# Values of four heads at a time: two weight tiles of 512 rows by 512 columns for each group of four

## The chip, the cores and the metric

The kernel runs on one core of a Trainium2 chip. The time is the device time of one execution in microseconds (us), and the number compared is the median of several executions. TensorE (PE) multiplies matrices; VectorE (DVE), ScalarE (ACT) and GpSimd (POOL) do the work on elements; SyncE (SP) issues the DMA transfers between the chip's main memory (DRAM here) and the on-chip memory. Each engine runs its own instructions in a fixed order and waits where a semaphore tells it to. TensorE writes its products to PSUM, which has eight banks of 128 x 512 float32.

## The reference, cut to what matters

512 tokens of 1024 numbers go through two layers (causal attention with forget gates, "fox", then retention), each with twelve heads of 128 and four heads that attend to a memory of 256 rows, and then through a second block: dilated attention in three groups of four heads, a causal convolution of 31 taps, gates, and a feed-forward part. Everything is float32.

```python
q, k, v, f_logit, q_mem, z = split_cols(h @ fox_w_in, [1536, 1536, 1536, 12, 512, 2048])
main = fox_attention(q, k, v, f_logit, fox_b_f)            # 12 heads of 128
...
q, k, v, q_mem, z = split_cols(h @ ret_w_in, [768, 768, 1536, 512, 2048])
main = retention(q, k, v)
...
q, k, v, glu_in, gates = split(h @ w_in, [1536, 3072, 4608, 6656])
for g, (window, dilation) in enumerate(((128, 1), (512, 4), (2048, 16))):
    o[g], m[g], l[g] = dilated_group_attention(q[4g:4g+4], k[4g:4g+4], v[4g:4g+4])
w = l * exp(m - max over groups of m)
a = sum(w * o) / sum(w)
```

The change concerns how the three matrices `v` are computed: 512 x 1024 times 1024 x 1536, once in each of the two layers and once in the second block.

## The kernel before

A float32 operand is held as the sum of two float32r arrays, hi and lo, and a product is three matmuls: hi by hi, hi by lo, lo by hi. Weights arrive in tiles of 1 MB at most. A tile lands in one of two buffers (`ring_w`, loaded from line 314), is split into hi (ACT, line 324) and lo (DVE, line 326) in one of two other buffers (`ring_hl`), and is then used by its "units": pieces of TensorE work of some 5.5 us. All other buffers of 128 x 512 come from two pools, `arena_r` for split and `arena_f` for whole operands. The driver (`run_jobs`) goes through the list of tiles. Before each unit it splits a piece of a coming tile (`cut_ahead`), and after it calls `run_bg`, which emits one step of the waiting background chains (two, if eight or more steps are pending, or if the rate is set to two) and one part of the convolution (up to six taps, line 1418 on DVE). A background chain is, for instance, the attention of one head: scores, exponentials, transposes, products with the values. So what a head's steps hide behind is given by the units that happen to follow. A scheduler may then still move instructions on each engine by its own estimate of times.

Products whose result is wanted with the tokens along the free dimension (queries, keys, gates) hold a 128 x 128 piece of weights and move 512 tokens (`mm3`, lines 213 to 215). Values are wanted the other way round, tokens on partitions. `add_nat` (lines 422 to 424) therefore holds a 128 x 128 piece of x and moves weights: for each tile of 1024 rows by 256 columns, that is two heads, four blocks of 128 tokens by eight row chunks by three, 96 matmuls of 256 columns in two units. The same helper computes the values of the memory heads. Fox calls it through `add_v` once for each of six pairs of heads (in `pair`), retention likewise (in `add_ret`), and the second block through `add_v2` for three groups by two pairs, all three at j = 0 and all three at j = 2 of the loop over the four heads j of a group.

In retention the chain of head h begins with `s1`, four products of the form 128 x 256 to 128 x 512 by two matmuls each (lines 1127 and 1128, the second with 64 rows only), and both heads of a pair are pushed at once.

In the second block head j of the three groups is joined by `push_softmax(j)`. The dilated groups hold the tokens in another order, so the row maxima and sums of all groups go through DRAM (`swap`, lines 1541, 1542, 1547 and 1548: `xn` carries the first group's numbers, `xp` the others'), then the weights of the groups are worked out on DVE (`coef`, lines 1554 to 1563), POOL multiplies the exponentials with them (line 1570), and only then TensorE transposes them (`tr`, line 1585) and multiplies by the values. The last scores before that are those of the first group (`scores_band`), four products by three matmuls on 128 x 256; line 1525 on DVE reads them. The values of the dilated groups go through DRAM too (`vdr`, stored from line 1676, loaded from line 1682).

## Time and profile before

| | before |
|---|---|
| median of 3 runs | 1933.24 us (1933.07 to 1943.24) |
| profiled execution, span | 1935.2 us |
| PE busy | 1880.0 us, 97%, 9759 matmuls |
| DVE busy | 1133.0 us, 59% |
| ACT busy | 826.5 us, 43% |
| POOL busy | 361.5 us, 19% |
| DMA | 194.57 MB, mean 101 GB/s |

The profile is of another execution than the three that were timed; its span, 1935.2 us, is the time that it shows for itself, and no other is given for it. A matmul's busy time is from its start to a modelled end, and neighbours overlap, so the time that a matmul takes is read from the distance between starts. The profile also has the clock that the chip granted to TensorE in each stretch, as a share of its full speed; a share between the two levels (0.50, that is 1.2 GHz, and 1.00, that is 2.4 GHz) is a mean over the stretch.

### The profile page before, as it was taken

The numbers are of one execution on the slowest core, as the hardware profiler recorded it, in microseconds if no ns is written. First come the engines' busy times: TensorE is split into PE (matmuls) and PEld (weight loads), VectorE is DVE, ScalarE is ACT, GpSimd is POOL, SyncE is SP. The second block draws the span as 40 slices with busy tenths as digits, with TensorE's granted clock in tenths as the row PEclk, the third lists the DMA queues.
The fourth block names the chain that finished last, engine by engine and source line by source line (L and its number), as shares of the span: only waits on it lengthen the run. The fifth ranks groups of instructions, "written<-read, shape, count | busy, mean of one in ns | idle before, by whom it ended". The sixth has DMA issues, their size and how long they took to land. (4 is left out here: it accounts for less than half of the span.)

```text
span 1935.2 us, 24633 instructions
## 1 busy us (share of the span) xinstructions
PE 1880.0 (97%) x9759; PEld 1594.7 (82%) x9759; DVE 1133.0 (59%) x1752; ACT 826.5 (43%) x1389; POOL 361.5 (19%) x348
## 2 busy tenths in 40 slices
PE   8999999999999999999999997999899999999998
PEld 7788888888888888888777986988788887888886
DVE  7644443443574564745469796868365387545555
ACT  6544343444445534445244333234353356433342
POOL 1110000111121223223351202020121232100101
PEclk9999999999999999999989998999999999999999
DMA  6341322223242222322223522353453222323221
GB/s 205 120 130 67 98 82 88 92 77 109 87 130 89 77 88 77 94 60 97 66 88 114 166 90 62 80 155 88 136 174 126 98 66 82 116 96 98 98 87 66
DMA packets 200373, 194.57 MB, mean 101 GB/s; under 512 B 22199, under 2 KB 171574, under 8 KB 200258
## 3 DMA queue, kind: packets, MB, share of 16 engines
q1 hardware_dynamic: 200258, 193.00, 32.0%
q8 instruction: 76, 1.25, 0.3%
q14 instruction: 39, 0.32, 0.1%
HBM read 182.40 MB, written 12.94 MB: 101 GB/s over the span
## 5 line engine op out<-in xcount | busy, mean ns | idle before, releaser
L213 PE MATMUL psum<-arena_r,ring_hl 128*128 128x512 f32 (+1 forms) x1936 | 750.1, 388 | 1.8 <-ACT arena_r L1904 1.3
L215 PE MATMUL psum<-arena_r,ring_hl 128*128 128x512 f32 (+1 forms) x1936 | 742.1, 384 | 5.1 <-DVE ring_hl L326 5.1
L214 PE MATMUL psum<-arena_r,ring_hl 128*128 128x512 f32 (+1 forms) x1936 | 742.5, 384 | 3.4 <-DVE arena_r L627 2.6
L326 DVE TENSOR_TENSOR ring_hl<-ring_w,ring_hl 128x1024 fp32r<-128x1024 f32 (+2 forms) x306 | 392.6, 1290 | 314.5 <-ACT ring_hl L324 303.6
L324 ACT CAST ring_hl<-ring_w 128x1024 fp32r<-128x1024 f32 (+2 forms) x307 | 316.1, 1037 | 504.3 <-PE psum L214 335.1
L215 PEld LDWEIGHTS psum<-arena_r,ring_hl 128*128 128x128 f32 x1936 | 367.1, 190 | 77.7 <-DVE ring_hl L326 6.3
L214 PEld LDWEIGHTS psum<-arena_r,ring_hl 128*128 128x128 f32 x1936 | 367.8, 190 | 73.7 <-DVE arena_r L627 3.3
L213 PEld LDWEIGHTS psum<-arena_r,ring_hl 128*128 128x128 f32 x1936 | 367.5, 190 | 73.1 <-issue 2.1
L422 PE MATMUL psum<-ring_hl,arena_r 128*128 128x256 f32 x640 | 183.3, 286 | 2.2 <-ACT ring_hl L324 2.2
L424 PE MATMUL psum<-ring_hl,arena_r 128*128 128x256 f32 x640 | 182.6, 285 | 0.3 <-DVE ring_hl L326 0.3
L423 PE MATMUL psum<-ring_hl,arena_r 128*128 128x256 f32 x640 | 182.5, 285 | 0.0
L1418 DVE SCALAR_TENSOR_TENSOR arena_f<-cpad,vec,arena_f 128x512 f32<-128x512 f32 x240 | 173.3, 751 | 1.7
L422 PEld LDWEIGHTS psum<-ring_hl,arena_r 128*128 128x128 f32 x640 | 124.2, 194 | 3.5 <-ACT ring_hl L324 2.6
L424 PEld LDWEIGHTS psum<-ring_hl,arena_r 128*128 128x128 f32 x640 | 124.1, 194 | 0.6 <-DVE ring_hl L326 0.6
L423 PEld LDWEIGHTS psum<-ring_hl,arena_r 128*128 128x128 f32 x640 | 124.1, 194 | 0.5
L206 DVE TENSOR_TENSOR arena_r<-psum,arena_r 128x512 fp32r<-128x512 f32 (+2 forms) x136 | 79.1, 605 | 71.3 <-ACT arena_r L205 71.1
L205 ACT CAST arena_r<-psum 128x512 fp32r<-128x512 f32 (+2 forms) x136 | 66.9, 526 | 85.0 <-PE psum L215 35.9
L205 ACT CAST arena_r<-arena_f 128x512 fp32r<-128x512 f32 (+1 forms) x78 | 46.2, 598 | 116.8 <-POOL arena_f L1950 67.3
L926 POOL TENSOR_SCALAR arena_f<-arena_f,small 128x512 f32<-128x512 f32 (+3 forms) x48 | 33.9, 726 | 307.9 <-DVE small L924 302.6
L206 DVE TENSOR_TENSOR arena_r<-arena_f,arena_r 128x512 fp32r<-128x512 f32 (+1 forms) x78 | 53.2, 688 | 59.8 <-ACT arena_r L205 59.1
L606 POOL TENSOR_TENSOR arena_f<-arena_f 128x512 f32<-128x512 f32 x40 | 63.6, 1602 | 109.1 <-ACT arena_f L601 106.8
L1950 POOL TENSOR_TENSOR arena_f<-arena_f 128x512 f32<-128x512 f32 x22 | 32.0, 1455 | 262.2 <-DVE arena_f L1926 252.2
(237 smaller groups left out, 2099.3 us busy)
## 6 DMA issues: line engine op xcount, KB each, us to landing
ring_w<-in_fox_w_in SPq DMA_DIRECT2D x28, 1024.0 KB
ring_w<-in_w_in SPq DMA_DIRECT2D x22, 1024.0 KB
ring_w<-in_w_up SPq DMA_DIRECT2D x22, 1024.0 KB
ring_w<-in_w_out SPq DMA_DIRECT2D x20, 1024.0 KB
ring_w<-in_ret_w_in SPq DMA_DIRECT2D x16, 1024.0 KB
ring_w<-in_w_in SPq DMA_DIRECT2D x24, 512.0 KB
ring_w<-in_w_down SPq DMA_DIRECT2D x10, 1024.0 KB
ring_w<-in_w_mem_kv SPq DMA_DIRECT2D x8, 1024.0 KB
```

The costliest lines, as they stand in the source:

```text
L205: nc.scalar.copy(h, src)
L206: nc.vector.tensor_sub(l, src, h.bitcast(F32))
L213: nc.tensor.matmul(ps, wh, xh, start=start and k == 0, stop=False, **o)
L214: nc.tensor.matmul(ps, wh, xl, start=False, stop=False, **o)
L215: nc.tensor.matmul(ps, wl, xh, start=False, stop=stop and k == n - 1, **o)
L324: nc.scalar.copy(j.hv[sl], v[sl])
L326: (nc.gpsimd if j.done in j.spare else nc.vector).tensor_sub(lo, v[sl], j.hv[sl].bitcast(F32))
L422: nc.tensor.matmul(o, c.h[:, sl], h[:, k, :], start=k == 0, stop=False)
L423: nc.tensor.matmul(o, c.l[:, sl], h[:, k, :], start=False, stop=False)
L424: nc.tensor.matmul(o, c.h[:, sl], l[:, k, :], start=False, stop=k == n - 1)
L606: nc.gpsimd.tensor_add(acc, acc, t.ap)
L1418: nc.vector.scalar_tensor_tensor(t, src, wk, t, ALU.mult, ALU.add)
```

## The change

A new helper `add_wide` computes the values of four heads from two tiles of 512 rows by 512 columns (1 MB each, as before). A matmul holds the same 128 x 128 piece of x and moves 512 columns of weights. The products of the four token blocks, 128 x 512 each, stay in four PSUM banks from the first tile to the second; each tile has two units of two token blocks, and those of the second tile copy the finished products out.

```diff
+    def add_wide(w, c0, x, evac):
+        d = {}
+        def unit(half, t0):
+            def f(h, l):
+                for t in (t0, t0 + 1):
+                    if not half:
+                        d[t] = PA.get()
+                    o, sl = d[t].ap, slice(t * P, (t + 1) * P)
+                    for k in range(4):
+                        c = x()[4 * half + k]
+                        nc.tensor.matmul(o, c.h[:, sl], h[:, k, :], start=not half and k == 0, stop=False)
+                        nc.tensor.matmul(o, c.l[:, sl], h[:, k, :], start=False, stop=False)
+                        nc.tensor.matmul(o, c.h[:, sl], l[:, k, :], start=False, stop=half == 1 and k == 3)
+                    if half:
+                        evac(t, d[t])
+                        d[t].free()
+            return f
+        for half in range(2):
+            all_jobs.append(
+                Job([((A, A, A), wsrc(w, half * 512, 512, c0, 512))], (4, 512), CUTO, [unit(half, 0), unit(half, 2)])
+            )
...
-            add_v(w, 3072 + p * 256, p)
+            if p % 2 == 0:
+                add_v(w, 3072 + p * 256, p // 2)
...
-                add_v(w, 1536 + p * 256, p); add_call(fin); z()
+            if p % 2 == 0:
+                add_v(w, 1536 + p * 256, p // 2)
+            add_call(fin)
+            z()
...
-    vdr = dpool.tile([2, 2, S, 256], F32, name="vdr")
+    vdr = dpool.tile([2, S, 512], F32, name="vdr")
...
+        def ev_dil(t, ps):
+            u = FS.get()
+            nc.scalar.copy(u.ap, ps.ap)
+            nc.sync.dma_start(vdr[g - 1, t * P : (t + 1) * P], u.ap)
+            u.free()
+        add_wide(w2, 3072 + 4 * g * P, getx, ev_dil if g else ev)
+    def load_v2(jp):
+        for g in (1, 2):
+            G[("v", g, jp)] = v = [FS.get(), FS.get()]
+            src = vdr[g - 1, :, jp * 256 : (jp + 1) * 256].rearrange("(p r) c -> p r c", r=4)
+            for i in range(2):
+                nc.sync.dma_start(v[i].ap.rearrange("p (r c) -> p r c", r=2), src[:, 2 * i : 2 * i + 2, :])
...
+                if j == 0:
+                    for g in (1, 2, 0):
+                        add_v2(g)
                 if j % 2 == 0:
-                    for g in (1, 2, 0):
-                        add_v2(g, jp)
+                    add_call(lambda jp=jp: load_v2(jp))
                 add_call(lambda j=j: push_softmax(j))
```

Eighteen tiles of values become nine pairs of such tiles, with as many bytes and as many splits. In fox and retention the even pairs of heads now have two value tiles and the odd ones none; in the second block all six are at j = 0, and only the loads of the values from DRAM are left at j = 2. `pv` and `pv_band` take their columns from other tiles, with matmuls of the same form. The memory heads keep `add_nat`. The other lines of the diff take out comments.

This moves work on TensorE in two places. The first is retention, at the scores of heads 0 and 1 (`s1`, lines 1127 and 1128, which are 1153 and 1154 after the change). Before:

```order
L782 MATMUL psum<-ident,arena_f 128x128 x8
L1127 MATMUL psum<-arena_r 128x512
L1128 MATMUL psum<-arena_r 128x512
L1127 MATMUL psum<-arena_r 128x384
L1128 MATMUL psum<-arena_r 128x384
L1127 MATMUL psum<-arena_r 128x256
L1128 MATMUL psum<-arena_r 128x256
L1127 MATMUL psum<-arena_r 128x256
L1128 MATMUL psum<-arena_r 128x256
L213 MATMUL psum<-arena_r,ring_hl 128x512
```

and of the change, from the middle of head 0's scores on:

```order
L1153 MATMUL psum<-arena_r 128x256
L1154 MATMUL psum<-arena_r 128x256
L1153 MATMUL psum<-arena_r 128x512
L1154 MATMUL psum<-arena_r 128x512
L1153 MATMUL psum<-arena_r 128x384
L1154 MATMUL psum<-arena_r 128x384
L1153 MATMUL psum<-arena_r 128x256
L1154 MATMUL psum<-arena_r 128x256
L1153 MATMUL psum<-arena_r 128x256
L1154 MATMUL psum<-arena_r 128x256
L213 MATMUL psum<-arena_r,ring_hl 128x512
```

Head 1's scores now follow those of head 0 with nothing between: sixteen such matmuls in a row where there were eight. Of the six pairs, two stood so before (heads 2 and 3, heads 6 and 7), and five do now (all but heads 10 and 11).

The second place is the second block at j = 2, behind the last scores of the first group (products of `arena_r` alone, 128x256). Before, the value tiles follow:

```order
L213 MATMUL psum<-arena_r 128x256
L214 MATMUL psum<-arena_r 128x256
L215 MATMUL psum<-arena_r 128x256
L422 MATMUL psum<-ring_hl,arena_r 128x256
L423 MATMUL psum<-ring_hl,arena_r 128x256
L424 MATMUL psum<-ring_hl,arena_r 128x256
```

and of the change, the projections that come next in the list:

```order
L213 MATMUL psum<-arena_r 128x256
L214 MATMUL psum<-arena_r 128x256
L215 MATMUL psum<-arena_r 128x256
L213 MATMUL psum<-arena_r,ring_hl 128x512
L214 MATMUL psum<-arena_r,ring_hl 128x512
L215 MATMUL psum<-arena_r,ring_hl 128x512
```

Between these scores and the transposes of `tr` there were 240 matmuls of values and 120 of projections at j = 0 and at j = 2, and 96 of projections at j = 1 and at j = 3. Now there are 264 of values and 120 of projections at j = 0, and 96 of projections at each of j = 1, 2 and 3.

## Rows read from the trace of the kernel before

**Rows 1.** The page, part 1: busy time, share of the span, instructions.
```profile
PE 1880.0 (97%) x9759; PEld 1594.7 (82%) x9759; DVE 1133.0 (59%) x1752; ACT 826.5 (43%) x1389; POOL 361.5 (19%) x348
```
**Rows 2.** Waits of PE: us in total, times, longest.
```profile
PE psum L1585 <- POOL arena_f L1570: 17.9, 4, 8.7
```
**Rows 3.** Groups by form: busy us, mean ns of one, then idle before.
```profile
L422 PE MATMUL psum<-ring_hl,arena_r 128*128 128x256 f32 x640 | 183.3, 286 | 2.2 <-ACT ring_hl L324 2.2
...
L2036 PE MATMUL psum<-ring_hl,arena_r 128*128 128x512 f32 x172 | 67.1, 390 | 0.0
```
**Rows 4.** Timeline of PE: start us, duration us; moving weights, 256 and 512 columns.
```profile
232.45 0.28 PE L422 MATMUL psum<-ring_hl,arena_r 128*128 128x256 f32 x1
...
235.93 0.28 PE L424 MATMUL psum<-ring_hl,arena_r 128*128 128x256 f32 x1
...
1690.18 0.39 PE L2036 MATMUL psum<-ring_hl,arena_r 128*128 128x512 f32 x1
...
1692.90 0.39 PE L2036 MATMUL psum<-ring_hl,arena_r 128*128 128x512 f32 x1
```
**Rows 5.** Timeline of PE at `tr` of j = 1, 2, 3; idle time before in brackets.
```profile
1195.64 1.11 PE L1585 MATMUL psum<-ident,arena_f 128*128 128x128 f32 x4 [8.66 <-POOL arena_f L1570]
...
1298.26 1.03 PE L1585 MATMUL psum<-ident,arena_f 128*128 128x128 f32 x8
...
1367.96 1.12 PE L1585 MATMUL psum<-ident,arena_f 128*128 128x128 f32 x4 [6.92 <-POOL arena_f L1570]
```
**Rows 6.** Timelines of SP, DVE and POOL: the swaps of j = 1 and j = 2.
```profile
1165.57 0.36 SPq L1541 DMA_DIRECT2D xn<-small  x1
...
1187.72 0.16 DVE L1554 TENSOR_TENSOR small<-small 128x4 f32<-128x4 f32 x1 [14.58 <-DMA small<-xn]
...
1192.50 8.11 POOL L1570 TENSOR_SCALAR arena_f<-arena_f,small 128x128 f32<-128x128 f32 x10 [0.88 <-ACT ring_hl L324]
...
1245.81 0.46 SPq L1541 DMA_DIRECT2D xn<-small  x1
...
1269.15 6.87 POOL L1570 TENSOR_SCALAR arena_f<-arena_f,small 128x256 f32<-128x256 f32 x10 [0.71 <-ACT ring_hl L324]
```
**Rows 7.** Windows after both waits: busy us of PE, PEld, DVE, ACT, POOL; clock; DMA.
```profile
1195.00:1200.00 5.00, 2.32 (x9) 1.93 (x10) 4.86 (x7) 0.59 (x2) 5.00 (x7) 0.50 0.00 0
1200.00:1205.00 5.00, 5.00 (x14) 3.84 (x14) 4.82 (x7) 0.58 (x1) 2.27 (x3) 0.55 0.65 210
...
1365.00:1370.00 5.00, 1.76 (x7) 1.37 (x8) 1.71 (x2) 0.59 (x1) 5.00 (x10) 0.50 0.67 212
1370.00:1375.00 5.00, 5.00 (x21) 4.11 (x20) 0.00 (x0) 0.59 (x1) 1.01 (x3) 0.82 0.76 290
```
**Rows 8.** Windows of retention, columns as in rows 7.
```profile
720.00:725.00 5.00, 5.00 (x14) 2.26 (x12) 2.66 (x5) 2.45 (x5) 2.72 (x3) 0.82 0.57 196
725.00:730.00 5.00, 5.00 (x12) 3.52 (x12) 1.27 (x3) 1.13 (x3) 3.12 (x4) 0.50 0.24 68
...
835.00:840.00 5.00, 5.00 (x15) 2.83 (x16) 3.55 (x8) 2.97 (x6) 3.90 (x4) 0.93 0.33 113
840.00:845.00 5.00, 5.00 (x18) 3.98 (x17) 0.14 (x1) 1.05 (x1) 1.91 (x3) 0.73 0.39 105
...
766.00:771.00 5.00, 5.00 (x19) 3.19 (x18) 2.30 (x6) 2.04 (x4) 4.50 (x5) 1.00 0.59 211
...
925.00:930.00 5.00, 5.00 (x16) 3.23 (x16) 2.53 (x7) 1.61 (x4) 3.94 (x4) 0.80 0.07 24
```
**Rows 9.** Timelines of PE and POOL: the last head of retention.
```profile
959.83 0.94 PE L220 MATMUL psum<-ones,arena_f 128*128 128x1 f32 x8
...
963.37 2.04 POOL L251 TENSOR_TENSOR arena_r<-ident,small 128x512 fp32r<-128x512 f32 x2 [0.35 <-DVE small L247]
```
**Rows 10.** The page, part 5: taps of the convolution and splits of weights.
```profile
L326 DVE TENSOR_TENSOR ring_hl<-ring_w,ring_hl 128x1024 fp32r<-128x1024 f32 (+2 forms) x306 | 392.6, 1290 | 314.5 <-ACT ring_hl L324 303.6
...
L1418 DVE SCALAR_TENSOR_TENSOR arena_f<-cpad,vec,arena_f 128x512 f32<-128x512 f32 x240 | 173.3, 751 | 1.7
```

More of the change, by code (lines that the diff above doesn't have):

```diff
@@ L936, in s4 @@
             def s4():
[L937 to L938 removed]
+                o = pv(G[("v", h // 4)], h % 4, d["pt"], d["p33"])
                 if h % 2:
                     G.pop(("own", h // 2)).free()
[L941 removed]
+                if h % 4 == 3:
+                    for x in G.pop(("v", h // 4)):
                         x.free()
@@ L1019, in add_fox, with add_v, ev @@
         add_call(lambda: (drain(), free_h()))
-    def add_v(w, c0, p):
-        def ev(b, ps):
-            if b == 0:
+    def add_v(w, c0, q):
+        def ev(t, ps):
+            if t < 3:
                 v = hl()
                 evac_hl(ps.ap, v.h, v.l)
-                G[("v", p)] = [v]
             else:
-                u, last = RS.get(), FS.get()
-                evac_hl(ps[:, 0:256], u[:, 0:256], u[:, 256:512])
-                nc.scalar.copy(last[:, 0:256], ps[:, 256:512])
-                G[("v", p)] += [u, last]
-        add_nat(w, c0, getx, ev)
+                v = FS.get()
+                nc.scalar.copy(v.ap, ps.ap)
+            G.setdefault(("v", q), []).append(v)
+        add_wide(w, c0, getx, ev)
     def tr_causal(p, p33):
@@ L1052, in tr_causal, with pv @@
         return r
-    def pv(v, odd, pt, p33):
+    def pv(v, i, pt, p33):
         ps = PA.get()
-        c = slice(odd * P, odd * P + P)
-        c2 = slice(256 + odd * P, 256 + odd * P + P)
-        v0, u, last = v
+        c = slice(i * P, i * P + P)
+        v0, v1, v2, last = v
         n1, n2, lo = slice(0, 384), slice(0, 256), slice(256, 512)
         mm3(ps.ap, [(v0.h[:, c], v0.l[:, c], pt[0].h, pt[0].l)], stop=False)
-        mm3(ps[:, 128:512], [(v0.h[:, c2], v0.l[:, c2], pt[1].h[:, n1], pt[1].l[:, n1])], start=False, stop=False)
-        mm3(ps[:, 256:512], [(u[:, c], u[:, c2], pt[2][:, n2], pt[2][:, lo])], start=False, stop=False)
+        mm3(ps[:, 128:512], [(v1.h[:, c], v1.l[:, c], pt[1].h[:, n1], pt[1].l[:, n1])], start=False, stop=False)
+        mm3(ps[:, 256:512], [(v2.h[:, c], v2.l[:, c], pt[2][:, n2], pt[2][:, lo])], start=False, stop=False)
         nc.tensor.matmul(ps[:, 384:512], last[:, c], p33, start=False, stop=True)
@@ L1610, in mul @@
             else:
-                pv_band(v, j % 2, pt, ps)
-            if j % 2:
-                for x in G.pop(("v", g, j // 2)):
+                pv_band(v, j, pt, ps)
+            if j % 2 if g else j == 3:
+                for x in v:
                     x.free()
```

46 lines of the change are left out of this document (11 added, 35 removed).

## The prediction

> **What bounds the kernel now.** I read the page first: TensorE is busy for 1880.0 of 1935.2 us, DVE for 59% [rows 1]. So nearly every microsecond that TensorE's own instructions take is on the path, and other engines matter only where TensorE waits for them or where its clock falls. Second, the waits of TensorE: the largest is at `tr` in the second block, on POOL's weighting (line 1570), four times and 17.9 us together [rows 2]. The reader should see in the timeline that they belong to j = 1 and j = 3, while j = 2 came without any [rows 5]. Third, the windows, for stretches in which TensorE is busy and yet slow because its granted clock is below 1.00 [rows 7, 8].
>
> **Part 1: matmuls of 512 columns instead of 256.** `add_nat` runs 1920 matmuls of 256 columns, 640 on each of three lines of which one is shown [rows 3]; 64 on each line are the memory heads', which stay. The 1728 of the eighteen value tiles become 864 of 512 columns. The mean of 286 ns is a modelled duration that overlaps the next one, so I take the distance between starts [rows 4]. From 232.45 to 235.93 lie 29 steps of 256 columns: 0.1200 us each. From 1690.18 to 1692.90 lie 12 steps of the same form with 512 columns (weights moving, activations held): 0.2267 us each. Two narrow ones cost 240.0 ns, a wide one 226.7. Saved: 1728 x 0.1200 - 864 x 0.2267 = 207.4 - 195.9 = 11.5 us. Both forms stand in this trace at full clock, so this term is the firmest.
>
> The Trainium skill speaks against it (TensorE: Matmul & The Clock Gate, Back-to-back issue gap). There, spacing in the fast state is the columns at 2.4 GHz plus about 2.5 ns, so joining two matmuls would save 2.5 ns, an estimate of 2.2 us for 864. The trace disagrees: its distances differ by 13.3 ns per pair, and the trace decides. By the page the sum below would be 9.3 us higher.
>
> **Part 2: the swap at j = 2 loses its cover.** Between the last scores of the first group and `tr` there stood 240 matmuls of values and 120 of projections at j = 2; after the change 96 of projections are left, as at j = 1 and j = 3. That cover is 96 x 0.2267 = 21.8 us against 240 x 0.1200 + 120 x 0.2267 = 56.0. What it has to cover is the way of the maxima and sums through DRAM, two writes and two reads of `xn` one after the other, then `coef` on DVE (which waits 14.58 us for a read at j = 1, with convolution taps queued behind it), then line 1570. From the first write to the start of line 1570 this took 26.9 us at j = 1 (1165.57 to 1192.50) and 23.3 at j = 2 (1245.81 to 1269.15) [rows 6], longer than 21.8 already; the first transposes of j = 1 came 3.1 us after that start. With the cover of j = 1 and j = 3, j = 2 will wait as they do.
>
> The wait, from both sides: j = 1 waited 8.66 and j = 3 6.92 us, and their second waits add 17.9 - 8.66 - 6.92 = 2.3 together [rows 2, 5], so at most 11.0. At the least, j = 2's own chain was 3.6 us shorter than j = 1's: 8.66 - 3.6 = 5.1. Behind each wait the clock is at 0.50 and comes back only after some matmuls: lost is the busy time times what lacks of the clock, at j = 1 2.32 x 0.50 + 5.00 x 0.45 = 3.4 us, at j = 3 1.76 x 0.50 + 5.00 x 0.18 = 1.8 [rows 7]. So 6.9 to 14.4. I take 10, between j = 3 (8.7 to 11.0) and the shorter own chain. At j = 0 the cover only grows, and there was no wait.
>
> **Part 3: retention, scores of two heads back to back.** TensorE is busy all the time there, but its clock is not always full. In the trace twice sixteen of these matmuls stood in a row, and both times the clock fell: to 0.82 and 0.50 in the two windows from 720, to 0.93 and 0.73 in those from 835. That lost 5.00 x (0.18 + 0.50) = 3.4 and 5.00 x (0.07 + 0.27) = 1.7 us [rows 8]. Of the eight heads that stood alone seven kept 1.00 (the window at 766 is one); the eighth, at 925, stood right behind the eight narrow matmuls of `stat_mm` and fell to 0.80. The change makes five rows of sixteen out of two, because the odd pairs lost their value units and the even ones moved theirs ahead of both heads. Three new ones at the mean of 2.55 us: 7.7; at the ends 5.1 and 10.2. The case at 925 may go or stay (1.0 us in the row shown); I leave it out.
>
> The Trainium skill ties a loss of the fast clock to gaps in which TensorE idles (TensorE: Matmul & The Clock Gate, Why this matters for your kernels). By that, sixteen matmuls without a gap would cost nothing, and the sum would be 7.7 lower. In this trace the two windows from 720 are at 0.82 and 0.50 with TensorE busy for 5.00 of 5.00 us.
>
> **Part 4: the end of retention.** The last head's normalisation goes from `stat_mm` on TensorE over POOL and DVE to the diagonal blocks of line 251, which the next broadcast (line 261) needs: 959.83 + 0.94 to 963.37 + 2.04 is 4.6 us [rows 9]. After the change 12 matmuls stand between, 2.7 us; with 1.9 uncovered. Bounds: 0, if POOL is free earlier, and 4.6. At the end of fox ten matmuls cover a similar gating step; I take nothing there and count it in the upper end.
>
> **At nothing.** Bytes, tiles and splits are as many as before, so loads and splits keep their pace behind the units. The copies out of PSUM have as many elements and hide behind the next units. Four banks are held over two tiles, which leaves four for a head's steps; the largest step takes three, and steps come a unit apart. If that cover failed, a step would wait for a unit, 24 x 0.2267 = 5.4 us, once per pair of tiles. On SP the value stores and loads move from j = 2 to j = 0 and behind j = 1; TensorE waited for none of them at j = 2.
>
> **Sum.** -11.5 + 10 + 7.7 + 1.9 = +8.1 us. The terms come from the profiled execution of 1935.2 us, which is 0.1% above the median of 1933.24; a difference carries over. 1933.24 + 8.1 = **1941 us**. With each term at its ends: -11.5 + 6.9 + 5.1 + 0 = +0.5 and -11.5 + 14.4 + 10.2 + 4.6 = +17.7, that is 1934 to 1951.
>
> **Rivals.** A: the three new rows of sixteen keep the clock: -11.5 + 10 + 1.9 = +0.4, 1934 us. For it: two cases are few, one of them cost only 1.7, and where the other small products lie will shift. It is what the page named in part 3 would have. B: neither the clock falls in retention nor does j = 2 wait in full, because scheduler and DRAM traffic let the swap end within 21.8 us: -11.5 + 0 to 5 + 0 to 1.9, 1922 to 1929 us, middle 1925. Against it: no swap in the trace after j = 0 was that short. C, on the other side: DVE becomes late in the second block. Where a unit brings one part of the convolution (6 taps x 0.751 = 4.5 us) and one split (1.29) [rows 10], DVE needs 5.8 us for a unit of 24 x 0.2267 = 5.4 us of TensorE. At j = 2 the longer units of values gave it time; now they are at j = 0. From the point at which DVE has no idle time left but its wait for `xn`, `coef` stands one part later in each of the swaps of j = 1, 2 and 3: 3 x 4.5 = 13.5 more, 1955 us. Against it: about as many splits and taps per unit stood at j = 1 and j = 3. D: what a matmul takes beyond its columns grows with the columns, so that a wide one takes two narrow ones' 0.2400 us and part 1 saves nothing: 1941 + 11.5 = 1953 us. The two distances of rows 4, each steady over a dozen steps or more, speak against it. (By the page named in part 1, which saves 2.2 us, it would be 1951.)
>
> **How the numbers follow.** The forecast 0.48, A 0.19, B 0.18, C 0.12, D 0.03. A measurement of this kernel can tell about 0.5% from no change, that is 1923.6 to 1942.9 us. Faster: the lower half of B, 0.09, and 0.02 for what I may have overpriced besides, taken from the forecast: 0.11. The same: the rest of B, A, and 0.26 of the forecast, whose terms reach to both sides of 1942.9: 0.54. Slower: 0.20 of the forecast, C and D: 0.35. The range takes in B, A and the forecast with its ends, 1922 to 1952, and leaves out C.
>
> **What would show it.** Part 1: the wide matmuls start 0.227 us apart. Part 2: a wait of 5 to 11 us at `tr` of j = 2 and a clock near 0.5 behind it, so waits on line 1570's counterpart of 23 to 29 us in all. Part 3: windows below 1.00 at five pairs of heads in retention. Part 4: a wait of about 2 us at the last broadcast of retention. The prediction is wrong if j = 2 shows no wait, if the clock stays at 1.00 in retention, or if a new wait of over 3 us stands elsewhere.

## The result

The changed kernel takes 1969.65 us (median of four runs, 1960.35 to 1976.01), the kernel before 1933.15 in the same comparison. The ratio of the comparison is 1.0164, 95% interval 1.0134 to 1.0195: slower by 1.6% (the two medians alone would give 1.0189), and outside the range of the prediction, whose upper end was 1952. The profiled execution of the change has a span of 1973.1 us against 1935.2, so its profile shows 37.9 us to be explained. It is one of the two longer executions of the four (1975.2 and 1976.0; the others took 1964.1 and 1960.4).

Where they are is read from matched instructions in the two timelines of TensorE: the statistics at the end of fox, the transposes and statistics of retention, the first matmul of each j's dilated scores in the second block (at j = 0 of the second of its two groups), and the statistics of the convolution's normalisation. "Beyond the work" is what a stretch lost when the matmuls that were saved or moved are taken into account (0.64 us saved for each value tile; three tiles of wide values more at j = 0, three narrow ones fewer at j = 2).

| stretch | before, us | after, us | difference | beyond the work | forecast |
|---|---|---|---|---|---|
| start to the end of fox | 537.4 | 533.7 | -3.7 | +0.1 | 0 |
| to the transposes of retention's second memory head | 74.6 | 77.5 | +2.9 | +2.9 | 0 |
| to the end of retention | 386.4 | 398.8 | +12.4 | +16.2 | +9.6 |
| to the dilated scores of j = 0 | 54.4 | 53.9 | -0.5 | -0.5 | 0 |
| j = 0 | 98.1 | 136.3 | +38.2 | +7.5 | 0 |
| j = 1 | 76.9 | 74.8 | -2.1 | -2.1 | 0 |
| j = 2 | 97.2 | 84.4 | -12.8 | +21.8 | +10 |
| j = 3 | 83.0 | 86.6 | +3.6 | +3.6 | 0 |
| the rest | 527.2 | 527.1 | -0.1 | -0.1 | 0 |

Beyond the work 49.4 us were lost; the forecast had 19.6. The page of the changed kernel (part 1, answering to [rows 1]) shows that TensorE was busy for 1886.1 us, 6.1 more than before, though it has 864 matmuls fewer; its stretches of low clock, shown below, took more than the matmuls gave:

```profile
PE 1886.1 (96%) x8895; PEld 1559.8 (79%) x8895; DVE 1133.9 (57%) x1746; ACT 831.3 (42%) x1381; POOL 366.6 (19%) x348
```

The waits of TensorE (us in total, times, longest) answer to [rows 2]. The transposes of `tr`, line 1609 now, wait six times instead of four, and 39.6 us instead of 17.9; the second row is new:

```profile
PE psum L1609 <- POOL arena_f L1594: 39.6, 6, 17.2
PE psum L448 <- DVE ring_hl L326: 5.3, 1, 5.3
```

**The wide matmuls.** In the timeline of TensorE (start, duration) sixteen steps from 307.83 to 311.46 are 0.2269 us each, as the forecast had them:

```profile
307.83 0.39 PE L446 MATMUL psum<-ring_hl,arena_r 128*128 128x512 f32 x1
...
311.46 0.39 PE L447 MATMUL psum<-ring_hl,arena_r 128*128 128x512 f32 x1
```

**The wait at j = 2.** The same timeline at `tr` of j = 1, 2 and 3, against [rows 5]:

```profile
1243.24 1.11 PE L1609 MATMUL psum<-ident,arena_f 128*128 128x128 f32 x4 [6.99 <-POOL arena_f L1594]
...
1328.30 1.11 PE L1609 MATMUL psum<-ident,arena_f 128*128 128x128 f32 x4 [17.23 <-POOL arena_f L1594]
1331.67 1.11 PE L1609 MATMUL psum<-ident,arena_f 128*128 128x128 f32 x4 [2.26 <-POOL arena_f L1594]
...
1406.28 1.11 PE L1609 MATMUL psum<-ident,arena_f 128*128 128x128 f32 x4 [10.82 <-POOL arena_f L1594]
```

j = 2 waits 17.2 and 2.3 us where the forecast had 5 to 11, and more than j = 1 and j = 3, which have the same cover of 96 matmuls. The chain behind it, against [rows 6], in the timelines of DVE, SP and POOL (idle time before in brackets):

```profile
1288.81 3.11 DVE L1442 SCALAR_TENSOR_TENSOR arena_f<-cpad,vec,arena_f 128x512 f32<-128x512 f32 x4
1291.83 0.42 DVE L1549 CUSTOM_DVE_ANT_0 arena_f<-psum,arena_f 128x256 f32<-128x256 f32 x1
...
1294.88 0.53 SPq L1565 DMA_DIRECT2D xn<-small  x1
...
1308.74 0.16 DVE L1578 TENSOR_TENSOR small<-small 128x4 f32<-128x4 f32 x1 [9.77 <-DMA small<-xn]
...
1316.05 0.33 SPq L1571 DMA_DIRECT2D small<-xn  x1
...
1319.31 0.28 DVE L1583 TENSOR_TENSOR small<-small 128x12 f32<-128x12 f32 x2 [6.80 <-DMA small<-xn]
1319.50 0.75 DVE L1442 SCALAR_TENSOR_TENSOR arena_f<-cpad,vec,arena_f 128x512 f32<-128x512 f32 x1
...
1320.97 0.68 DVE L1415 TENSOR_TENSOR cpad<-psum,arena_f 128x512 f32<-128x512 f32 x1
...
1321.71 1.22 DVE L326 TENSOR_TENSOR ring_hl<-ring_w,ring_hl 128x1024 fp32r<-128x1024 f32 x1
...
1325.44 10.66 POOL L1594 TENSOR_SCALAR arena_f<-arena_f,small 128x128 f32<-128x128 f32 x12
```

The way through DRAM, from the first write (1294.88) to the issue of the last read (1316.05), is 21.2 us, hardly less than at j = 1 before (22.4). Two other pieces are long. The last matmul of the scores started at 1289.00 on TensorE, but DVE first had four taps of the convolution (line 1442) to do and read them at 1291.83; the write left 5.9 us after that matmul, where at j = 1 and j = 3 it was 0.7 and 0.8. And between the last read and POOL's line 1594 lie 9.4 us, where before had 4.5 at j = 1: taps, a split of weights and an evacuation stand between the small steps of `coef`. From the last scores to the weighting it is 36.4 us in all, against 27.6 at j = 1 before (0.7, 22.4 and 4.5).

**Retention.** The windows at the three pairs of heads that newly stand sixteen in a row, columns as in [rows 7] (answering to [rows 8]):

```profile
665.00:670.00 5.00, 5.00 (x15) 3.07 (x15) 2.77 (x7) 2.77 (x7) 4.27 (x5) 0.89 0.00 0
670.00:675.00 5.00, 5.00 (x18) 3.98 (x17) 0.00 (x0) 0.00 (x1) 1.58 (x2) 0.77 0.37 107
...
780.00:785.00 5.00, 5.00 (x12) 3.04 (x12) 2.26 (x5) 1.88 (x4) 5.00 (x6) 0.66 0.00 1
785.00:790.00 5.00, 5.00 (x16) 3.91 (x15) 0.00 (x0) 0.00 (x0) 0.43 (x1) 0.66 0.37 105
...
895.00:900.00 5.00, 5.00 (x13) 2.86 (x14) 3.19 (x8) 2.64 (x6) 4.63 (x5) 0.76 0.15 57
900.00:905.00 5.00, 5.00 (x14) 3.85 (x14) 1.58 (x1) 0.00 (x0) 2.17 (x2) 0.55 0.39 105
```

Busy time by what lacks of the clock is 1.7, 3.4 and 3.4 us: 8.5, where the forecast had 7.7.

**j = 0.** A wait that the forecast did not have. First SP's issues of the swap, before and then after:

```profile
1073.88 0.36 SPq L1541 DMA_DIRECT2D xn<-small  x1
1082.62 1.08 SPq L1547 DMA_DIRECT2D small<-xn  x2
```

```profile
1082.42 0.41 SPq L1565 DMA_DIRECT2D xn<-small  x1
1092.83 0.32 SPq L1571 DMA_DIRECT2D small<-xn  x1
1093.24 0.39 SPq L1565 DMA_DIRECT2D xn<-small  x1
1102.61 0.32 SPq L1571 DMA_DIRECT2D small<-xn  x1
```

Before, both writes (the other at 1071.13) went out ahead of both reads, and the reads were issued 11.5 and 12.2 us after the first write (the line shows both as one). Now they are write, read, write, read in SP's order, as at j = 1 to 3 in both kernels, and take 20.2 us to the issue of the last read, where it was 12.2. DVE, in order, stands at `coef` for it, and then TensorE for DVE:

```profile
1102.67 0.17 DVE L1583 TENSOR_TENSOR small<-small 128x12 f32<-128x12 f32 x1 [7.29 <-issue]
...
1106.49 0.17 DVE L1583 TENSOR_TENSOR small<-small 128x12 f32<-128x12 f32 x1 [2.17 <-DMA small<-xn]
...
1110.71 1.21 DVE L326 TENSOR_TENSOR ring_hl<-ring_w,ring_hl 128x1024 fp32r<-128x1024 f32 x1
...
1111.98 0.79 PE L448 MATMUL psum<-ring_hl,arena_r 128*128 128x512 f32 x1 [5.29 <-DVE ring_hl L326]
```

Between 1106.49 and the split at 1110.71 that TensorE needed, DVE did the rest of `coef` with a tap after nearly every small step.

### The profile page after: what moved, and what is told of

Its sections match the earlier page's. It is cut to its first block, busy times and chain, and to the rows that moved or that the text cites. A ratio compares the mean times of both kernels' runs of the same rounds, so it can differ in the third digit from the quotient of the medians.

```text
span 1973.1 us, 22899 instructions
## 1 busy us (share of the span) xinstructions
PE 1886.1 (96%) x8895; PEld 1559.8 (79%) x8895; DVE 1133.9 (57%) x1746; ACT 831.3 (42%) x1381; POOL 366.6 (19%) x348
## 5 line engine op out<-in xcount | busy, mean ns | idle before, releaser
L448 PE MATMUL psum<-ring_hl,arena_r 128*128 128x512 f32 x288 | 113.1, 393 | 5.3 <-DVE ring_hl L326 5.3
L446 PE MATMUL psum<-ring_hl,arena_r 128*128 128x512 f32 x288 | 113.3, 393 | 0.0
L447 PE MATMUL psum<-ring_hl,arena_r 128*128 128x512 f32 x288 | 112.9, 392 | 0.0
L205 ACT CAST arena_r<-arena_f 128x512 fp32r<-128x512 f32 (+1 forms) x78 | 46.1, 597 | 119.0 <-POOL arena_f L1974 67.3
L632 POOL TENSOR_TENSOR arena_f<-arena_f 128x512 f32<-128x512 f32 x40 | 63.7, 1603 | 95.9 <-ACT arena_f L627 93.6
L2060 PE MATMUL psum<-ring_hl,arena_r 128*128 128x512 f32 (+1 forms) x180 | 69.4, 385 | 0.0
L2062 PE MATMUL psum<-ring_hl,arena_r 128*128 128x512 f32 (+1 forms) x180 | 69.3, 385 | 0.0
L2061 PE MATMUL psum<-ring_hl,arena_r 128*128 128x512 f32 (+1 forms) x180 | 69.2, 384 | 0.0
```

The source lines that it names most:

```text
L205: nc.scalar.copy(h, src)
L446: nc.tensor.matmul(o, c.h[:, sl], h[:, k, :], start=not half and k == 0, stop=False)
L447: nc.tensor.matmul(o, c.l[:, sl], h[:, k, :], start=False, stop=False)
L448: nc.tensor.matmul(o, c.h[:, sl], l[:, k, :], start=False, stop=half == 1 and k == 3)
L2060: nc.tensor.matmul(o, x.h[:, sl], h[:, k, cs], start=k == 0, stop=False)
```

## Experiments

All ratios are against the kernel before on the same chip, with 95% intervals. Two theories stood against each other: that the three places (fox, retention, second block) lose separately and for the reasons above; and that they act on each other through shifted loads, so that a part alone costs little.

**Fox alone.** Wide tiles in the first layer; retention and the second block keep `add_nat`. `add_vw` is the change's wide `add_v` under another name.

```diff
-            add_v(w, 3072 + p * 256, p)
+            if p % 2 == 0:
+                add_vw(w, 3072 + p * 256, p // 2)
```

> Only the first layer (fox) computes its values in tiles of 512 columns; retention and the second block are as before. Separate costs (my theory): six tiles' worth of matmuls at 0.64 us each saved, 3.8 us, and nothing else but at most the 2.8 us that the changed kernel lost to a fallen clock around 560 to 570 us: 1929 to 1932 us. Rival (the parts act on each other, so that a part alone costs little): also about 1929. The traces of before and of the change already show 537.4 against 533.7 us at the end of fox, so more than 1934 would be against both.

Measured: 0.9994 (0.9979 to 1.0009). In its profile the statistics at the end of fox stand at 533.3 us. Both theories allow this, and the ratio by itself cannot tell a gain of 0.2% from none. The profiles can: over all eighteen the median of that place is 534.2 us in the eight with wide tiles in fox and 537.8 in the ten without. So the matmuls' gain is there, and four banks held over two tiles cost nothing that shows in that layer.

**Retention alone.** The same edit in `add_ret`.

> Only retention has the wide tiles. Its heads' scores stand sixteen in a row five times, as in the changed kernel. Separate costs: -3.8 for the matmuls, +11.7 for the windows of low clock that the changed kernel has beyond before, +3 for waits, so +11 to +13: 1944 to 1946 us. Rival (the low clock in retention comes from an earlier start of the layer, or from the whole program): within 4 us of before, 1929 to 1937.

Measured: 1.0083 (1.0060 to 1.0106), 16 us on a median of before of 1936. Retention loses by itself; the rival falls. It is somewhat more than expected.

**Retention alone, rows of eight.** The odd head's chain begins with an empty step.

```diff
-                push(push_head(2 * p + 1))
+                push([nop] * 1 + push_head(2 * p + 1))
```

> As the run with wide tiles in retention alone, but the odd head's chain begins with one empty step, so that its scores come a unit after the even head's: rows of eight, sixteen only once. My theory (the row of sixteen is what lets the clock fall): the low windows go, all but one or two, also before's own two; -3.8, less 5 for before's two, and up to 4 for waits at the end: 1926 to 1933 us. Rival (the clock falls because the value units are gone from the odd pairs, not because of the row): the clock windows stay, 1941 to 1946.

Measured: 1.0023 (1.0005 to 1.0041), 10.7 us less in the median than the run without the step. The windows at the places where the scores now lie, eight and eight:

```profile
665.00:670.00 5.00, 5.00 (x20) 3.17 (x18) 1.72 (x4) 2.57 (x4) 0.03 (x1) 1.00 0.66 210
675.00:680.00 5.00, 5.00 (x22) 3.43 (x21) 3.87 (x5) 4.16 (x6) 0.09 (x1) 1.00 0.04 7
...
775.00:780.00 5.00, 5.00 (x19) 3.18 (x18) 2.85 (x6) 2.03 (x4) 0.70 (x1) 1.00 0.63 210
```

The clock is full at all ten rows of eight, of which three are shown, with the value units placed as in the change. So the row of sixteen, not the missing value units, lets the clock fall. The time is still above the 1926 to 1933 us expected: heads 10 and 11 now stood sixteen in a row and lost the clock at 915, and at the end of the layer TensorE waited for other things (line 220 for 5.0 us once, line 261 for 1.5).

**The second block alone.**

> Only the second block has the wide tiles, all at j = 0; the layers are as before. My theory (the swap at j = 2 has lost its cover, and the swap at j = 0 now has weight loads queued behind it): the changed kernel's losses in this block, 7.5 at j = 0, 21.5 at j = 2, 3.9 at j = 3, less 3.8 for the matmuls and about 1.6 at j = 1: +25 to +29, 1958 to 1962 us. The forecast's own size (a wait of 5 to 11 us at j = 2 and nothing at j = 0) would give 1936 to 1944. Rival (the long waits come from the layers' changes having shifted the phase of the convolution and the loads): also 1936 to 1944.

Measured: 1.0083 (1.0063 to 1.0102), 1950.8 us, less than my theory expected and more than the rival. The wait at j = 2 is there without any change in the layers, 14.39 and 2.26 us. The wait at j = 0 is not: the swap goes write, read, write, read there too, but line 448 waits only 1.7 us in all. So what DVE has queued behind `coef` depends on when things come: beyond the work j = 0 lost 2.2 us here, and 7.5 in the profile of the whole change. The ratios of the three parts alone add up to +1.6% (-0.0006 + 0.0083 + 0.0083), which is that of the whole. Their profiles do not: the second block, from retention's last statistics to those of the convolution, took 409.5 us before, 425.7 here and 436.0 in the whole change. So of the 37.9 us that the profile of the change shows, some 10 in the second block stand in no part alone, and for them the theory that the parts act on each other is not refuted. The two shorter executions of the change may lack them; they have no profile.

**More cover.** In the second block alone, two empty steps more in the chain of the swap, so that the transposes come 10.9 us of matmuls later (16.3 at j = 2).

```diff
-            swap, nop, weigh, nop, lambda: (tr(1), tr(2)), lambda: (mul(1), mul(2)), lambda: tr(0), lambda: mul(0),
+            swap, *[nop] * 2, weigh, *[nop] * 2, lambda: (tr(1), tr(2)), lambda: (mul(1), mul(2)), lambda: tr(0), lambda: mul(0),
```

> The second block wide as in the run before, and two empty steps more in the chain of the swap (one ahead of the weighting, one behind it), so that 48 more matmuls of 512 columns (72 at j = 2) stand between the last scores and the transposes: 10.9 us of cover (16.3 at j = 2). My theory (the waits are a cover of 22 us that is too short for a chain of 28 to 37): the waits at j = 1 and j = 3 go, that of j = 2 falls below 3 us, and with them the low clock behind: 33 us of waits and some 7 of clock less, 1910 to 1920 us against 1951 of the run without the steps. Rival (the chain is held up by work of TensorE or by the driver's pace, so that it moves back with the transposes): the waits stay, 1945 or more.

Measured: 1.0023 (1.0008 to 1.0038), 12 us less than without the steps but more than 18 us above what was expected. The waits of TensorE in its profile:

```profile
PE psum L214 <- DVE arena_r L206: 9.8, 2, 9.0
PE psum L1611 <- POOL arena_f L1596: 8.5, 4, 3.1
```

The waits at `tr` fell from 33.0 to 8.5 us, but a new one of 9.8 stands at a query or key that DVE had not copied out in time. Neither theory had that.

**The kernel before with more cover.** The same two steps in the kernel before and nothing else.

> The kernel before, with nothing but the two empty steps more in the chain of the swap. My theory: its waits at j = 1 and j = 3, 17.9 us, and about 5 us of low clock behind them go, and j = 2 keeps cover enough: 1908 to 1916 us where before is 1933. Rival (a chain later by two units makes something after it late, the attention's output or the convolution's normalisation): 1925 or more.

Measured: 1.0065 (1.0040 to 1.0091): slower, a plain miss. The waits again:

```profile
PE psum L215 <- DVE ring_hl L326: 10.9, 7, 3.1
...
PE psum L1611 <- POOL arena_f L1596: 4.8, 2, 2.5
PE psum L213 <- ACT ring_hl L324: 4.7, 1, 4.7
PE psum L214 <- DVE arena_r L206: 4.6, 1, 4.6
```

The 17.9 us at `tr` fell to 4.8, which is 13.1 won; line 215 went from 5.1 to 10.9, with 4.7 and 4.6 new: 15.1 given back to the splits and copies of DVE and ACT. That accounts for no gain. The second block took 418.1 us against 409.5. Within it all waits of TensorE together grew by 3.0 us (20.1 to 23.1), and the busy time at low clock cost 15.5 us instead of 10.9 (busy time by what lacks of the clock): 7.6 of the 8.6 us.

**Without the taps.** If DVE is behind, then its convolution is what to take away. Two runs of one execution each, the second block wide and the kernel before, each with the first of the 31 taps only; the other thirty are left out, so their whole times (1930.7 and 1929.4 us) are compared with nothing.

```diff
-                for k in range(k0, k1):
+                for k in range(k0, min(k1, 1)):
```

> The second block wide, and of the convolution's 31 taps only the first is worked out (30 of 31 instructions for each of eight chunks on DVE are left out). It asks why the wait at j = 2 was 14 to 17 us and not the 5 to 11 of the forecast. If DVE's taps stand in the chain (reads of the scores late, and taps between the steps of the weights): from the last scores to the first write of the swap 1 us instead of 5.4, from the last read to POOL's weighting 4 to 5 instead of 9.4, and a wait of 4 to 8 us at j = 2. If it is the way through DRAM or SP's queue: a wait at j = 2 of 12 us or more all the same. The whole time says little, since 170 us of DVE work are gone: 1915 to 1945 us.

> The kernel before with 30 of the convolution's 31 taps left out, beside the run of the wide second block without them: what the lost cover at j = 2 costs when DVE is free. The waits at j = 1 and j = 3 should be as in that run (6.9 and 4.5 us), none at j = 2, and that run's 6.6 us at j = 2 then is the whole price of the cover. If the wide block has another cost besides, its other waits differ too. One look, so the whole time is not compared, but some 1915 to 1930 us.

Measured: at j = 2 of the wide second block without taps, timeline of TensorE:

```profile
1289.53 0.66 PE L1611 MATMUL psum<-ident,arena_f 128*128 128x128 f32 x4 [3.61 <-POOL arena_f L1596]
1293.14 1.11 PE L1611 MATMUL psum<-ident,arena_f 128*128 128x128 f32 x4 [2.96 <-POOL arena_f L1596]
```

6.6 us instead of 16.7. From the last scores to the first write it is 0.7 us instead of 5.4, from the last read to the weighting 4.2 instead of 9.4, while the way from the first write to the last read is 18.1 instead of 18.7. j = 1 waits 6.9 us, as much as j = 2. The kernel before without taps waits at j = 1 and j = 3 only, 12.5 us together, and

```profile
PE psum L1611 <- POOL arena_f L1596: 12.5, 4, 5.7
```

is its row. The clearest number is the length of the second block:

| | before | second block wide | difference |
|---|---|---|---|
| with the taps | 409.5 us | 425.7 us | +16.2 us |
| without the taps | 401.5 us | 402.9 us | +1.4 us |

The lost cover alone costs 6.6 us of wait and the clock behind it, less the matmuls' 3.8, and that is nearly nothing; some 15 of the 16 us need the convolution on DVE. (One profile each; in the profiles of before, fox alone, and the two of retention alone, whose second blocks are the same, its length is 409.5 to 411.3 us.)

**Taps held.** In the second block alone, no convolution for four units from the swap of j = 2 on.

```diff
-        if bg2:
+        if state.get("hold"):
+            state["hold"] -= 1
+        elif bg2:
             bg2.popleft()()
...
             n, r = stats(j, 0), stats(j, 1)
+            if j in (2,):
+                state["hold"] = 4
```

> The second block wide, and no part of the convolution emitted for four units from the swap of j = 2 on, so that ten taps less (7.6 us of DVE) stand ahead of the weights of j = 2 there, and come later. If DVE's taps make the wait at j = 2 long: it falls from 16.6 us to about 9, and the time by 6 to 9 us, to about 1942 where the run without holding was 1951. If the way through DRAM sets it: 15 us or more still, and the time is the same.

Measured: 1.0105 (1.0078 to 1.0132), no gain over 1.0083. The wait at j = 2 fell from 16.7 to 13.4 us, and that of j = 3 rose from 8.3 to 11.5:

```profile
1306.03 1.11 PE L1615 MATMUL psum<-ident,arena_f 128*128 128x128 f32 x4 [10.84 <-POOL arena_f L1600]
1309.69 1.12 PE L1615 MATMUL psum<-ident,arena_f 128*128 128x128 f32 x4 [2.54 <-POOL arena_f L1600]
...
1383.82 1.12 PE L1615 MATMUL psum<-ident,arena_f 128*128 128x128 f32 x4 [9.45 <-POOL arena_f L1600]
1386.96 1.12 PE L1615 MATMUL psum<-ident,arena_f 128*128 128x128 f32 x4 [2.02 <-POOL arena_f L1600]
```

The expected size (to about 9 us) was wrong; what was taken from one swap came back at the next.

**Both cures in the whole change** (rows of eight, two steps more).

> The whole change, with both cures: the odd head of a pair in retention begins a unit later, and the chain of the swap has two empty steps more. If the three causes (rows of sixteen in retention, the lost cover at j = 2, waits at j = 1 and 3 that before had already) are all there is: 1933 - 11.5 for the matmuls + 8 left in retention - 20 for the waits of before + up to 8 at j = 0 and j = 2, 1910 to 1920 us. If the four banks held, or the values made so early, cost something of their own: 1930 or more.

Measured: 1.0051 (1.0034 to 1.0068), better than the change by 1.1% and still slower than before. The 1910 to 1920 us rested on the waits falling away with nothing in their place. At `tr` they did fall, from 39.6 to 7.0 us, but TensorE now waits 8.8 us at line 214 for DVE's copies, 4.2 us more than the change at line 215 for its splits, and the clock still fell at the one row of sixteen that is left.

**Looking for a gain.** Fox wide, and the two rows of sixteen of before taken apart; then the same with four taps after a unit instead of six.

```diff
-                push(push_head(2 * p + 1))
+                push([nop] * (p in (1, 3)) + push_head(2 * p + 1))
```

> What is left as a gain: fox wide, retention and the second block as before, and in retention the odd head of the two pairs whose scores stand sixteen in a row begins a unit later. Matmuls -3.8, the low clock at the two rows -5 at most: 0.995 to 0.998 of before, if each row of sixteen costs what the traces showed (2.6 us on the mean). If the clock falls elsewhere instead: 0.998 to 1.001.

> As the run with fox wide and the rows apart, and four taps of the convolution after a unit instead of six, so that DVE is less behind when the swaps of the second block come, and the taps that are left run where DVE idles after j = 3. If DVE's lateness is part of the waits at j = 1 and j = 3 of the kernel before as well: 3 to 6 us less than that run, 0.992 to 0.996 of before. If the convolution then ends too late for its normalisation: 1.000 or more.

Measured: 0.9988 (0.9974 to 1.0002) and 1.0104 (1.0082 to 1.0125). The first has no low clock in retention at all in its profile and is the fastest complete kernel up to here; the interval does not tell it from the kernel before. The second was expected to help and lost: its waits at `tr` were 27.2 us and those for splits on line 215 13.8. Fewer taps after each unit spread the same work over more units, all of them beside swaps; that this is the reason was only argued.

**A shorter way through DRAM alone.** What was still open: the empty steps and the taps move DVE's work and the wait together. Here the second of the two round trips through `xn` (the sums) goes on another engine's queue, so that it need not follow the first; DVE's work stays as it is. POOL's queue in the second block alone, in the fastest kernel so far, and in the whole change with rows of eight; then ACT's.

```diff
-                nc.sync.dma_start(xn[j, k].rearrange("(i p) -> p i", p=P), n[:, c : c + 4])
+                (nc.gpsimd if k else nc.sync).dma_start(xn[j, k].rearrange("(i p) -> p i", p=P), n[:, c : c + 4])
...
-                nc.sync.dma_start(r[:, c : c + 4], xn[j, k].rearrange("(p r) -> p r", r=4))
+                (nc.gpsimd if k else nc.sync).dma_start(r[:, c : c + 4], xn[j, k].rearrange("(p r) -> p r", r=4))
```

> The second block alone with wide values, and of the swap's two round trips through xn the second (the sums) issued by POOL's queue instead of SP's, so that the two can run side by side; nothing is left out. In the run of the second block alone they ran one behind the other, 18 to 22 us from the first write to the last read, TensorE waited 33.0 us at the transposes, and the ratio was 1.0083. If the two round trips in series set the wait: first write to last read 10 to 13 us, the waits at j = 1 to 3 shorter by 7 to 10 us each (j = 2 from 16.7 to about 7, j = 1 and 3 to about 1), 1925 to 1937 us. If DVE's lateness sets it, as the two empty steps made it look: the waits fall by some 3 to 5 us each and come back at splits and copies of DVE (lines 214, 215), 1943 us or more.

> The fastest kernel so far (first layer wide, the two old rows of sixteen in retention taken apart, second block narrow; 0.9988) with the second round trip of the swap on POOL's queue; nothing is left out. Waits of TensorE at the transposes were about 18 us, all at j = 1 and 3. If the series of round trips sets them: they go to below 4 us, 1918 to 1924 us, a ratio of 0.991 to 0.994. If DVE does: 0.996 to 1.002, with the time back at lines 214 and 215.

> The whole change with an empty step between the rows of retention, and the second round trip of the swap on POOL's queue, no empty steps in the swap; nothing is left out. Without either cure the change is at 1.0164; the empty step in retention was worth 0.6%. If the series of round trips sets the waits at j = 0 to 3 (45 us with the wait at line 448): 1920 to 1935 us. If DVE does: 1945 us or more, as with the two empty steps in the swap (1943.1).

> As the run with POOL's queue, but the second round trip of the swap is issued by ACT; nothing is left out. ACT then stands at the read until the write has landed, some 9 us each time, with evacuations and splits behind it. If that is covered: the same time as with POOL's queue. If not: new waits of TensorE for ACT's splits (line 213) and copies of 3 to 8 us at each of four swaps, 1935 to 1960 us. It tells whether the queue may be any, or must be one with little work behind it.

Measured: 1.0098 (1.0076 to 1.0120), 0.9981 (0.9969 to 0.9993), 1.0094 (1.0079 to 1.0109) and 0.9986 (0.9975 to 0.9996). The timelines of SP and POOL at j = 2 of the first:

```profile
1276.64 0.53 SPq L1567 DMA_DIRECT2D xn<-small  x1
...
1288.68 0.33 SPq L1573 DMA_DIRECT2D small<-xn  x1
```

```profile
1278.90 0.80 POOL L1567 DMA_DIRECT2D xn<-small  x1 [17.72 <-ACT arena_f L1514]
1295.94 0.55 POOL L1573 DMA_DIRECT2D small<-xn  x1 [16.24 <-DMA xn<-small]
```

The two round trips now overlap, but each takes longer: 12.0 and 17.0 us from write to read, against 10.0 and 8.3 in series in the run on one queue. So at j = 2 the way is 19.3 us, not shorter than 18.7, the expectation (10 to 13) failed there, and the wait rose from 16.7 to 20.0. What a shorter way would give at j = 2, where the loss is, these runs do not tell. At j = 1 and j = 3 it did shrink, from 19.0 to 15.2 and from 20.7 to 17.8, but the waits at `tr` only went from 8.1 to 7.6 and from 8.3 to 7.0. In the fastest kernel it shrank by 6.3 us at both j = 1 and j = 3 (21.4 to 15.1, 21.1 to 14.8), and the waits by 1.0 and 2.5. Where the rest went stands in DVE's timeline at j = 1, the last wait for a read on one queue and then on two:

```profile
1183.01 0.28 DVE L1615 TENSOR_TENSOR small<-small 128x12 f32<-128x12 f32 x2 [4.97 <-DMA small<-xn]
```

```profile
1182.41 0.17 DVE L1610 TENSOR_TENSOR small<-small 128x4 f32<-128x4 f32 x1 [13.18 <-DMA small<-xn]
```

Counted from the last scores, DVE went on after 25.9 us with one queue and after 21.4 with two. But with one queue the first steps of `coef` and three taps between them ran between the two reads, and POOL's weighting began 1.1 us after the wait; with two all of `coef`, those taps included, came behind the wait, and the weighting began 4.6 us after it. So the wait at `tr` is made of both, the way through DRAM, for which DVE stands idle, and DVE's own work behind it; shortening the one by some microseconds left most of it. A really short way, of 2 or 3 us, could not be had by a queue alone and was not tried. Nor was the order of the source, both writes ahead of both reads, forced on one queue at j = 1 to 3: where it came about, first write to last read took 9.9 to 13.4 us in eight swaps (seven of them at j = 0) and 16.6 to 23.0 in three of the kernel before with more cover.

The intervals of the second and the fourth lie wholly below 1, so these are the kernels of the study that beat the kernel before, by 0.19 and 0.14%; their distance to 0.9988 on one queue is within the intervals. ACT's queue cost no more than POOL's, but its waits at `tr` were 19.3 us, no fewer than the 17.6 on one queue. The third, 1954.4 us, is on the side that its expectation gave to DVE (1945 or more), with the way at j = 2 again no shorter (19.6 us).

## Why the prediction was wrong

**Part 1 was right.** 0.2269 us per wide matmul against 0.2267; fox, where nothing else happens, came out at -3.7 against -3.84. Rival D, by which a wide step takes what two narrow ones take (0.2400 us), falls with the 0.2269. The Trainium skill (TensorE: Matmul & The Clock Gate, Back-to-back issue gap) gives its formula of 2.5 ns per matmul for a matmul by itself, and says of a stream that also loads weights, as this one does, that the formula counts too little for few columns; so it spoke less against the 13.3 ns than the prediction had it. The trace agrees at 256 columns (0.1200 us against an estimate of 0.1092 by the formula). For many columns the section says that it counts too much, and there the trace differs: 0.2269 against 0.2158.

**Part 2 had the right mechanism and less than half of the size, +21.8 against +10.** The step that failed is the size of the wait: I took the waits of j = 1 and j = 3 as the model for j = 2. The first wait there is 17.2 us where j = 1 before had 8.7, and its chain is 8.8 us longer (36.4 against 27.6): 5.2 more from the scores to the first write and 4.9 more from the last read to the weighting, with 1.3 less between. The first of these I left out, since I measured the swap from its first write; before, j = 2's shorter way through DRAM in [rows 6] already came with a later write, 3.7 us after the scores, which a row ahead of those would have shown. Both are DVE's lateness, and the run without taps takes them away (the waits go from 16.7 to 6.6 us). The way through DRAM is in the chain all the same, 21.2 of the 36.4 us; the second queue did not shorten it at j = 2, so its part is not told apart. The forecast was of a kernel whose DVE has time.

**Rival C had the mechanism that decided at j = 2, at 0.12.** Its point was that DVE has no idle time left but the wait for `xn`. At j = 1 that was so before the change already (61.7 us busy and 14.7 waiting, of 76.9); the change made it so at j = 2, and not at j = 3. Its price was off: the weighting began later by 5.6 us at j = 2 and by 3.2 at j = 3, counted from the last read (9.4 against 3.8, 8.0 against 4.8), and not at j = 1, where it had put 4.5 at each. Windows of whole stages: j = 2 of before, then j = 0 and j = 2 of the change:

```profile
1227.80:1325.00 97.20, 97.20 (x601) 87.63 (x600) 74.67 (x136) 32.54 (x64) 11.58 (x14) 1.00 0.46 125
```

```profile
1063.92:1200.20 136.28, 130.99 (x592) 108.82 (x593) 93.58 (x153) 42.25 (x69) 15.38 (x15) 0.96 0.41 123
...
1275.00:1359.40 84.40, 64.91 (x313) 54.37 (x312) 67.33 (x127) 27.58 (x55) 13.91 (x14) 0.88 0.34 74
```

Before, j = 2 was 97.2 us of TensorE over 74.7 of DVE. The value tiles bring TensorE much work and DVE little, so that was where DVE caught up. After, 64.9 us of TensorE stand over 67.3 of DVE, and the stage takes 84.4 us: DVE's work and its waits of 16.6 us for `xn` (9.77 and 6.80), one behind the other. The slack went to j = 0, where DVE is busy for 93.6 of 136.3 us and did as many taps as before, 82. The rival's argument against itself ("about as many splits and taps stood at j = 1 and j = 3") was the error: those stages lived on what j = 0 and j = 2 had cleared, as I read the windows; no run isolates it.

**Part 3 was right in mechanism and too small.** The three new rows of sixteen lost 8.5 us against 7.7. Over all eighteen profiles the clock fell at 27 of 31 rows of sixteen and at 7 of 154 rows of eight (all seven at head 10). What I left out came on the bad side: the old row at heads 6 and 7 lost 3.4 instead of 1.7, head 10 alone 3.2 instead of 1.7, and its scores waited 1.75 us for DVE. That is 11.7 us of clock in place of 7.7. Of retention's 16.2 us the rest is waits, among them 2.2 us at line 220 just before the statistics at its end, which the forecast did not have. The Trainium skill's rule that ties the loss of the fast clock to idle gaps (TensorE: Matmul & The Clock Gate, Why this matters for your kernels) does not cover these windows, in which TensorE is busy for all of 5.00 us.

**Part 4** showed 1.1 us of wait at lines 261 and 262 against 1.9, in its bounds.

**"At nothing" failed at j = 0.** I asked of SP's queue only whether TensorE waits for the transfers that move. The change also turned the order of the swap at j = 0 from two writes and two reads into write, read, write, read, which DVE waits for, and a split that TensorE needs stands behind that on DVE: 7.5 us. The prediction's "at j = 0 the cover only grows, and there was no wait" looked at `tr` alone. The question that was missing is what is queued behind each waiting instruction, on SP and on DVE, at its new place. The second block alone, with the same order and 1.7 us there, shows that it does not always cost as much.

**Not foreseen and not settled:** +2.9 us between the layers, where the clock fell behind a wait of 2.7 us that before had too, without the fall (that stretch takes 77.4 to 77.5 us in three of the eighteen profiles and 74.6 to 74.8 in the others); and +3.6 at j = 3, where the wait grew from 7.2 to 11.1 us with a chain that was longer by the 3.2 us named above and by 1.9 from the first write to the last read; in the second block alone it was 8.3. The changed kernel's runs also spread more (16 us) than those of before at that time (10 us), and no profile here tells why.

## What to carry to other kernels

A stretch in which the busiest engine has much to do and another little can be where the other catches up, as the windows of j = 2 read; work moved out of it takes that slack along, even if both engines' totals stay as they were. So cost a move per stage, with the demand of every engine in the stage it leaves and in the one it enters, and measure a chain that loses its cover from the last instruction of the covered work to the first that waits, with every engine's queue in it. When moving a wait's victim later gives back less than the wait took, as with the empty steps here (24.5 us of wait less for 12 us in the wide second block, 13.1 less for a loss in the kernel before), look for what another engine owes behind it.

## What the runs showed of the hardware

TensorE's granted clock can fall from 2.4 to 1.2 GHz while the engine is busy without a gap: sixteen small matmuls in a row (half of them with 64 rows of the array) did it 27 times in 31, eight 7 times in 154, and each fall cost 1.7 to 3.4 us here. An empty step between two groups of eight, which only changes what stands between them, kept the clock at 1.00. And a write of 512 numbers to DRAM and the read that waits for it took 7 to 12 us each time in the swaps on one queue, write, read, write, read; two of them in series, at j = 1 to 3, were 18 to 22 us with the convolution on DVE and 17 to 19 without it. Issued from two queues at once they did not simply halve that: 12.0 and 17.0 us side by side at j = 2.
